# Transposes of queries, keys, attention weights and merged rows by VectorE and DRAM, branch sums kept in PSUM, and a planned SyncE queue

## The chip, the cores and the metric

The kernel runs on one core of one Trainium2 chip. The metric is the device time of one execution in microseconds (us), median of the runs. TensorE (PE in the profile) multiplies matrices into PSUM, ScalarE (ACT) and VectorE (DVE) work on tiles of 128 partitions, GpSimd (POOL) and SyncE (SP) mostly issue transfers (DMA) between DRAM and the on-chip memory (SBUF).

## What is computed

One layer of a gated encoder: 512 tokens of width 2048, float32. All twelve attention heads are of width 128; three branches (A, B, C) have four heads each.

```python
hn = rmsnorm(x, norm_g)
proj = hn @ w_in                 # 2048 x 12292: q, k, v, gate of 12 heads,
                                 # 4 forget logits, 3 x 2048 merge gates
gates = sigmoid(merge columns + b_gate)
ya = softmax(qn kn^T + cumulated log forget, causal) v          # branch A
yb = softmax(qn kn^T + relative bias, 9 chunks of 64) v         # branch B
yc = stick-breaking(q k^T) v                                    # branch C
y  = [ya, yb, yc] * silu(gate)
merged = sum over branches of gates_n * (y_n @ w_up_n)          # 512 x 2048
out = x + merged @ w_out
```

qn and kn are q and k after a root-mean-square norm of each head (A and B only).

## The kernel before

**Products.** Each float32 operand is split into a high part that TensorE's fast format holds exactly and a low remainder (ACT makes the high part, L376, DVE the low, L386). A product is three fast matmuls, high by high, low by high, high by low; every one of them goes through `mm` (L266). A **unit** is the work on one weight tile of 256 rows by 512 columns: 12 matmuls of 128x128 by 128x512. There are 8 raw weight tiles in SBUF (NR), and the splits run LA = 2 units ahead.

**Strassen.** Two groups of 512 columns (one gate group and the q, k, v, gate of one head) are computed together by a seven-product Strassen scheme (class `Strassen`, L596 to L704; each product has 4 units, named by `PLAIN`, in the order 5, 1, 6, 7, 4, 2, 3). The weight sums of products 5 and 7 are made by DMAs that add into the tile (`add_up`, issued by POOL, L282); those of 6 and 3 by DVE (L588). Each product has its own pair of PSUM banks (one for each half of the tokens), of 4 in all (`accs`); four more banks serve attention (`atts`). What comes out is combined by DVE and ACT in SBUF (`after`, L649 to L704).

**Order of the whole.** First two groups (head C0 and gate group 0) are multiplied without Strassen, then 11 Strassen tasks run, one for each further head with a gate group, then the up projection (24 units of 24 matmuls, `up_units`), then the output projection (2 Strassen tasks, `out_task`).

**A head** (class `Head`). Its q, k, v and gate lie token by token and have to be laid out channel by channel: `turned` (L868 to L876) makes 4 TensorE transposes each for K and Q into an `atts` bank, from which ACT and DVE make the split parts (`qk`). The gate of all heads but the last goes another way (`gate`): DVE transposes blocks of 32x32 (L920), SP stores the tile to DRAM (L923), and ACT's queue fetches it back in pieces of 32 floats (L930). The scores (`soft_scores`, `stick_scores`, L261 to L263) are then made; the weights p are transposed on TensorE (`soft_trans`, L1019, 10 blocks a head), split, and multiplied by the values (`av`, L1107 to L1109). For the last head the mask is added by a small matmul (L988) and the steps stand closer together. The finished head is stored (`yd`) and fetched back in the up projection. The merged rows are transposed on TensorE too (`turned_m`, L1357, 4 groups of 16 blocks).

**Forget logits** are made on DVE (`forget_sums`) from x rows and weight rows fetched in 512-column pieces.

**The planner.** `Flow` simulates PE, ACT and DVE while the program is built: each step is a generator that yields events, slots (`t2s`, `atts`, `raws`...) or an engine with a cost; the earliest startable step goes next and steps that could start together go by due time. The three engines carry out their instructions in the order thus written. SP's queue is not planned: `fetch` and `stored` only estimate when a transfer lands (`landing`). `at(u, step)` lets a step begin at unit u; the offsets within a head stand in `OFF`.

Of the kernel before, what the change touches and what calls it, by code (L numbers as in the profile page):

```python
# [36 lines left out]
Q, K, V, G = 0, 1, 2, 3  # L37
PE, ACT, DVE = 0, 1, 2
# [19 lines left out]
class Task:  # L58
    def __init__(self, gen, slack, ready):
        self.gen, self.slack, self.ready = gen, slack, ready  # L60
        self.prev, self.fin = None, 0.0
        self.engine = self.cost = self.due = self.wait = None


class Flow:
# [5 lines left out]
    LATE = (0.3, 0.12, 0.12)  # L71

    def __init__(self):
        self.clock = [0.0] * 3
        self.idle = [0.0] * 3
        self.now = self.fin = 0.0
        self.tasks = []
# [12 lines left out]
    def advance(self, task):  # L90
        while True:
# [16 lines left out]
            elif isinstance(w[0], Slots):  # L108
                slots, n = w
                if len(slots.free) < n + (slots.kept if task.slack > 1 else 0):  # L110
                    return
                slots.free.sort()
                task.ready = max(task.ready, slots.free[n - 1])
# [11 lines left out]
    def run(self):  # L125
        while self.tasks:
            best = None
            for t in list(self.tasks):
                if t.engine is None:
                    self.advance(t)  # L130
            for t in self.tasks:
                if t.engine is not None:
                    key = (max(self.clock[t.engine], t.ready), t.due)
                    if best is None or key < best[0]:
                        best = key, t
# [4 lines left out]
            e = t.engine  # L140
            self.idle[e] += start - self.clock[e]
            self.now = start
# [21 lines left out]
def hybrid_kernel(  # L164
# [22 lines left out]
    pa = ctx.enter_context(tc.tile_pool(name="pa", bufs=4, space=PS))  # L187
    pt = ctx.enter_context(tc.tile_pool(name="pt", bufs=4, space=PS))
# [9 lines left out]
    t2s, atts, raws, xps = Slots(NT, KEPT), Slots(4), Slots(NR), Slots(NX)  # L198
    accs, wls = Slots(4), Slots(LA)
# [69 lines left out]
    line = [0.0, 0.0]  # L269
# [7 lines left out]
    def fetch(to, src, ready, kb):  # L277
        nc.sync.dma_start(to, src)
        return Event(landing(ready, kb))
# [28 lines left out]
    onef, zerof, nu_f = tmpc[:, blk(0)], tmpc[:, blk(1)], tmpc[:, blk(2)]  # L308
# [5 lines left out]
    identb = cp.tile([P, P], BF16, name="identb")  # L314
    nc.vector.tensor_copy(identb, identf)

    mska = cp.tile([P, P], BF16, name="mska")
    nc.gpsimd.affine_select(out=nu_f, in_=zerof, pattern=[[-1, P]], base=0, channel_multiplier=1,
                            compare_op=ALU.is_ge, fill=NEG)
    nc.vector.tensor_copy(mska, nu_f)  # L320

# [6 lines left out]
    for c in (0, 2):  # L328
# [3 lines left out]
    rstd = cp.tile([P, QB], F32, name="rstd")  # L332
    rstd_ev = Event()
# [4 lines left out]
                                                  mybir.EngineType.DVE}))  # L338
# [8 lines left out]
    class Unit:  # L347
# [7 lines left out]
        def load(self):  # L355
            for s in self.srcs:
                yield raws, 1
                self.raw = raw_tile(self.shape)
                self.there.t = fetch(self.raw, s, flow.ready, 256 * self.shape[0]).t
# [30 lines left out]
    def products(u, ps, kts, tbs, block, first=False, last=False, bank=None, done=None, outer=False):  # L390

        for group in [[tb] for tb in tbs] if outer else [tbs]:
            if bank is not None:
                for tb in group:
                    yield bank[0], 1
                    ps[tb] = bank[1]()
            for j, kt in enumerate(kts):
                for tb in group:
# [4 lines left out]
                    mm(ps[tb], h, u.hi[:, j, :], first and j == 0)  # L403
                    mm(ps[tb], lo, u.hi[:, j, :])
            yield u.ready
            for j, kt in enumerate(kts):
                for tb in group:
                    yield PE, mm_us(S)
                    mm(ps[tb], block(kt, tb)[0], u.lo[:, j, :], stop=last and j == len(kts) - 1)
# [75 lines left out]
    def norm_x():  # L485
# [11 lines left out]
        yield from rsqrt(rstd, m, D, tmp, QB)  # L497
        set_(rstd_ev)
# [54 lines left out]
    class Product(Unit):  # L553
# [6 lines left out]
        def load(self):  # L560
# [7 lines left out]
            ev = fetch(self.raw, task.src(*first, c), flow.ready, 512)  # L568
# [23 lines left out]
    PLAIN = [(p, c) for p in (5, 1, 6, 7, 4, 2, 3) for c in range(CH)]  # L592

    class Strassen:
# [9 lines left out]
        def __init__(self, src, ops, done, order=PLAIN, other=(), rest=None):  # L604
            self.src, self.ops, self.done, self.rest = src, ops, done, rest
            self.order, self.other = order, other
            self.ps, self.ev = {}, {}
            self.v, self.u, self.u2, self.u3 = ([None, None] for _ in range(4))
# [8 lines left out]
        def mms_of(self, p, c):  # L617
            own = [x for q, x in self.order if q == p]
            first, last = c == own[0], c == own[-1]
            slots, new = (atts, att) if p in self.other else (accs, acc)  # L620

            def go(u):
                ps = self.ps.setdefault(p, [None, None])
                if first:
                    yield slots, 2
                    ps[:] = new(), new()
                yield from products(u, ps, (2 * c, 2 * c + 1), (0, 1), self.ops[p], first, last,
                                    done=lambda tb: self.after(p, tb, slots), outer=last)
            return go

        def left(self, name, tb, op):
# [6 lines left out]
            yield fetch(r, self.rest(name, tb), flow.now, 256)  # L638
# [5 lines left out]
        def after(self, p, tb, slots):  # L644
            ps = self.ps[p][tb]
            v, u, u2, u3 = self.v, self.u, self.u2, self.u3
# [6 lines left out]
            if p in (1, 5):  # L653
                yield t2s, 1
                c = t2("v" if p == 5 else "u")
                yield ACT, act_us(S)
                nc.scalar.activation(c, ps, AF.Copy)
                (v if p == 5 else u)[tb] = c
                give(slots)
# [914 lines left out]
```

## Time and profile before

| | |
|---|---|
| median of 3 runs | 1300.71 us (1300.23 to 1301.82) |
| the profiled execution's span | 1300.1 us |
| instructions | 17368 |
| granted TensorE clock | 1.000 |
| busy: PE, DVE, ACT, POOL | 1294.1, 1069.5, 748.2, 92.0 us |
| moved by DMA | 284.39 MB |
| matmuls of 512 columns through L266 | 5328 |
| other TensorE instructions | 613 |

Busy time is the union of an engine's instructions. Matmuls are pipelined: one of 512 columns is shown about 390 ns long, but the next starts 227 ns after it. In the chain of what ended last each matmul counts only until the next one starts, so that chain gives the cost of an instruction in the stream. The DMA share is the mean busy share of the core's 16 DMA engines; the queues are q1 (issued by SP), q10 (by ACT) and q0 (by POOL).

### The profile page before, as it was taken

The numbers are of one execution on the slowest core, as the hardware profiler recorded it, in microseconds if no ns is written. First come the engines' busy times: TensorE is split into PE (matmuls) and PEld (weight loads), VectorE is DVE, ScalarE is ACT, GpSimd is POOL, SyncE is SP. The second block draws the span as 40 slices with busy tenths as digits, with TensorE's granted clock in tenths as the row PEclk, the third lists the DMA queues.
The fourth block names the chain that finished last, engine by engine and source line by source line (L and its number), as shares of the span: only waits on it lengthen the run. The fifth ranks groups of instructions, "written<-read, shape, count | busy, mean of one in ns | idle before, by whom it ended". The sixth has DMA issues, their size and how long they took to land.

```text
span 1300.1 us, 17368 instructions
## 1 busy us (share of the span) xinstructions
PE 1294.1 (100%) x5941; PEld 1075.1 (83%) x5941; DVE 1069.5 (82%) x1607; ACT 748.2 (58%) x1259; POOL 92.0 (7%) x116
## 2 busy tenths in 40 slices
PE   9999999999999999999999999999999999999998
PEld 8888888888888888888888888888888888888887
DVE  7966797898989888898886886978879668698767
ACT  7745465565557646576466664666658546463442
POOL 0001000110011001110011000110000000000110
PEclk9999999999999999999999999999999999999999
DMA  9855687896788989888787777877796756738983
GB/s 358 256 147 145 185 230 194 230 239 215 218 238 237 250 236 272 236 240 240 205 249 175 222 213 191 252 162 208 224 282 194 264 194 196 177 93 258 250 245 126
DMA packets 124072, 284.39 MB, mean 219 GB/s; under 512 B 34368, under 2 KB 40144, under 8 KB 123984
## 3 DMA queue, kind: packets, MB, share of 16 engines
q1 hardware_dynamic: 83328, 221.42, 50.7%
q0 software_dynamic: 14976, 54.53, 23.1%
q10 hardware_dynamic: 25680, 7.34, 2.3%
q8 instruction: 46, 0.75, 0.2%
q14 instruction: 42, 0.34, 0.1%
HBM read 260.66 MB, written 22.59 MB: 218 GB/s over the span
## 4 chain that ended last, share of the span: by engine, by line
PE 99%; DMA 1%; DVE 0%; issue 0%; ACT 0%; ACTq 0%
PE acc L266 93%; PE att L1019 1%; PE att L873 1%; DMA gl<-u 1%; PE att L1109 1%; PE att L1108 1%; PE att L261 1%; PE att L262 1%; PE att L263 1%; PE att L1357 1%; PE att L1107 1%; PE att L430 0%; DVE s L702 0%; DVE u L1161 0%; DVE gt L920 0%
## 5 line engine op out<-in xcount | busy, mean ns | idle before, releaser
L376 ACT ACTIVATE wh<-raw 128x1024 fp32r<-128x1024 f32 (+1 forms) x404 | 426.9, 1057 | 412.6 <-PE acc L266 317.6
L386 DVE TENSOR_TENSOR wl<-raw,wh 128x1024 fp32r<-128x1024 f32 (+1 forms) x405 | 492.6, 1218 | 159.1 <-PE acc L266 110.6
L266 PE MATMUL acc<-wh,x 128*128 128x512 f32 x1664 | 428.7, 392 | 0.1
L266 PEld LDWEIGHTS acc<-wh,x 128*128 128x128 f32 x1664 | 310.2, 188 | 62.8 <-issue 0.3
L266 PE MATMUL acc<-wh,t 128*128 128x512 f32 x1056 | 272.4, 391 | 0.0
L266 PE MATMUL acc<-wl,x 128*128 128x512 f32 x832 | 230.7, 391 | 0.0
L266 PEld LDWEIGHTS acc<-wh,t 128*128 128x128 f32 x1056 | 197.1, 188 | 40.3
L266 PEld LDWEIGHTS acc<-wl,x 128*128 128x128 f32 x832 | 155.4, 188 | 32.3 <-DVE wl L386 0.2
L266 PE MATMUL acc<-wl,t 128*128 128x512 f32 x528 | 148.0, 392 | 0.0
L282 POOL DMA_DIRECT2D raw<-in_w_col x88 | 76.1, 865 | 867.6 <-ACT wh L376 209.0
L588 DVE TENSOR_TENSOR raw<-raw,raw 128x1024 f32<-128x1024 f32 x104 | 126.4, 1218 | 0.1
L266 PEld LDWEIGHTS acc<-wl,t 128*128 128x128 f32 x528 | 98.3, 188 | 19.7
L266 PE MATMUL acc<-wh,m 128*128 128x512 f32 x448 | 112.9, 389 | 0.0
L266 PE MATMUL acc<-wh,y 128*128 128x512 f32 x384 | 103.1, 390 | 0.0
L266 PEld LDWEIGHTS acc<-wh,m 128*128 128x128 f32 x448 | 84.1, 188 | 17.4
L266 PEld LDWEIGHTS acc<-wh,y 128*128 128x128 f32 x384 | 72.0, 188 | 15.0
L266 PE MATMUL acc<-wl,m 128*128 128x512 f32 x224 | 62.5, 390 | 0.0
L266 PE MATMUL acc<-wl,y 128*128 128x512 f32 x192 | 59.5, 391 | 0.0
L266 PEld LDWEIGHTS acc<-wl,m 128*128 128x128 f32 x224 | 41.9, 188 | 8.8 <-DVE wl L386 0.2
L266 PEld LDWEIGHTS acc<-wl,y 128*128 128x128 f32 x192 | 35.8, 188 | 7.1
L247 ACT ACTIVATE ah<-att 128x512 fp32r<-128x512 f32 (+3 forms) x48 | 20.9, 436 | 31.7 <-PE att L1019 31.6
L1323 DVE TENSOR_TENSOR sg<-acc,sg 128x512 f32<-128x512 f32 x48 | 32.9, 690 | 5.0 <-PE acc L266 2.6
(182 smaller groups left out, 1119.9 us busy)
## 6 DMA issues: line engine op xcount, KB each, us to landing
raw<-in_w_col SPq DMA_DIRECT2D x235, 512.0 KB, 5.0
raw<-in_w_col POOLq DMA_DIRECT2D x88, 512.0 KB, 8.2
raw<-in_w_out SPq DMA_DIRECT2D x40, 512.0 KB, 4.1
raw<-in_w_up SPq DMA_DIRECT2D x24, 512.0 KB, 3.8
sg<-gl SPq DMA_DIRECT2D x48, 256.0 KB, 4.8
xf<-in_xn SPq DMA_DIRECT2D x32, 256.0 KB, 6.7
raw<-in_w_out POOLq DMA_DIRECT2D x16, 512.0 KB, 6.5
gl<-u SPq DMA_DIRECT2D x22, 256.0 KB, 9.9
```

The costliest lines, as they stand in the source:

```text
L247: nc.scalar.activation(hi, src, AF.Copy)
L261: nc.tensor.matmul(ps, lh, rh, start=start, stop=False, skip_group_check=more)
L262: nc.tensor.matmul(ps, lh, rl, start=False, stop=False, skip_group_check=more)
L263: nc.tensor.matmul(ps, ll, rh, start=False, stop=stop, skip_group_check=more)
L266: nc.tensor.matmul(ps, w, x, start=start, stop=stop, skip_group_check=more)
L282: nc.gpsimd.dma_start(to, src, accum_op=ALU.add)
L376: nc.scalar.activation(u.hi, u.raw, AF.Copy)
L386: nc.vector.tensor_sub(u.lo, u.raw, f(u.hi))
L588: nc.vector.tensor_add(to.raw, to.raw, self.raw)
L873: nc.tensor.transpose(ps[:, blk(tb)], self.c[tb][:, blk(r)], identf)
L1019: nc.tensor.transpose(ps[:, blk(i)], self.p[i][:, blk(j)], identf)
L1323: nc.vector.tensor_mul(t, ps[tb], t)
```

## The change

1. **q, k, gate** of every head go the way the gate went: DVE transposes 32x32 blocks in the 384 columns q, k, gate of each of 4 token tiles (`crossed`), SP stores the four tiles (values with them), and SP fetches K, Q and the gate back, each by four DMAs in pieces of 32 floats (`back`); the values come back by one DMA. `turned` and its TensorE transposes are gone.
2. **Attention weights**: DVE transposes p in place (`sent`), SP stores it, and `soft_in` fetches the four column blocks back by four DMAs each. `soft_trans` is gone.
3. **Merged rows**: groups 0, 2 and 1 of 4 go the same way (`folded`, `turned_m`); the last, 3, stays on TensorE (`spun_m`).
4. **Strassen sums in PSUM**: products 6, 7 and 4 are added by TensorE into the banks that hold product 1, product 3 into those of product 5. ACT copies the bank after 1 and after 6, and the next product on it waits (`gate`) for that copy. Order 5, 1, 6, 7, 2, 3, 4. Banks: 6 `accs`, 2 `atts`.
5. **SP is planned** as a fourth engine: each fetch and store yields SP with a cost, and SP carries out its queue in the planned order. A step takes a slot only when it is free to within 0.5 us.
6. **Order**: heads C0 and C1 come first without Strassen; the last Strassen task holds two gate groups instead of the last head; offsets in a head are longer; the mask matmul is gone. The up projection takes branches A of groups 0 and 2 later.
7. **Forget logits** in 8 pieces of 256 columns, all four heads at once: 32 fetches of 256 KB instead of 48, and 128 DVE sums of 256 columns instead of 64 of 512.

```diff
-    pa = ctx.enter_context(tc.tile_pool(name="pa", bufs=4, space=PS))
-    pt = ctx.enter_context(tc.tile_pool(name="pt", bufs=4, space=PS))
+    pa = ctx.enter_context(tc.tile_pool(name="pa", bufs=6, space=PS))
+    pt = ctx.enter_context(tc.tile_pool(name="pt", bufs=2, space=PS))
...
     def landing(ready, kb):
-        line[0] = max(line[0], ready) + 0.5
-        line[1] = max(line[1], line[0] + 1.0) + kb / 370.0
-        return line[1] + 1.5
+        line[0] = max(line[0], ready + 1.0) + kb / 370.0
+        return line[0] + (LAND if ready > 20.0 else 1.6)
+    def store(to, t, kb, slots=None, n=1):
+        yield SP, 0.37
+        nc.sync.dma_start(to, t)
+        ev = Event(landing(flow.fin, kb))
...
+    def back(to, src):
+        n = src.shape[0] * 4
+        for b in range(4):
+            yield SP, 0.54
+            nc.sync.dma_start(to[32 * b:32 * (b + 1), :].rearrange("p (n c) -> p n c", c=32),
+                              src.rearrange("t (a r) c -> (t a) r c", r=32)[:, :, 32 * b:32 * (b + 1)]
+                              .rearrange("n r c -> r n c"))
+        return Event(landing(flow.fin, n * 32) + PIECES)
     def add_up(to, src, ready, kb):
         nc.gpsimd.dma_start(to, src, accum_op=ALU.add)
-        line[1] += kb / 250.0
-        return Event(max(line[1], ready) + 6.5)
+        line[0] += kb / 250.0
+        return Event(max(line[0], ready) + 6.5)
...
+            opens = p in (5, 1, 2)
+            key = {3: 5, 6: 1, 7: 1, 4: 1}.get(p, p)
+            after = {6: 1, 7: 6, 3: 5, 4: 7}.get(p)
             def go(u):
+                ps = self.banks.setdefault(key, [None, None])
+                gate = (lambda tb: self.event(after, tb)) if first and not opens else None
...
+            if p in (1, 6):
                 yield t2s, 1
+                t = (u if p == 1 else u2)[tb] = t2("u")
                 yield ACT, act_us(S)
+                nc.scalar.activation(t, w, AF.Copy)
                 set_(self.event(p, tb))
...
+        def crossed(self):
...
+            for tb in range(QB):
+                yield DVE, dve_us(3 * P) + 0.07
+                c = self.c[tb]
+                nc.vector.transpose(c[:, :3 * P], c[:, :3 * P])
+                ev = yield from store(d[tb], c, 256, t2s)
+            self.event("x").t = ev.t + LATER
+        def qk_in(self, r):
+            yield self.event("x")
...
+            yield (yield from back(t, self.d[:, :, blk(r)]))
+            if self.n == C:
+                yield from split(h, lo, t, S)
...
+        def sent(self, i):
+            yield self.event("s", i)
...
+            nc.vector.transpose(p, p)
+            self.gone[i] = (yield from store(self.pd[i, :, :m], p, m / 2)).t
+        def soft_in(self, j):
+            for i in range(j, QB):
+                yield self.event("d", i)
+            yield Event(max(self.gone) + LATER)
...
+            yield (yield from back(f(lo), self.pd[j:, :, blk(j)]))
+            yield from split(h, lo, f(lo), n, self.event("a", j))
...
-OFF = dict(cs=4, ct=12, co=14, s=8, t=14, o=16, s1=3, t1=4, o1=5)
-FAT, FGAP, FLATE = 44, 15, 3.5
+UPS = [(0, 0), (0, 1), (2, 0), (2, 1), (0, 2), (2, 2)] + [(g, b) for g in (1, 3) for b in range(3)]
+DRAMS = (0, 2, 1)
+EARLY = 0.5
+LAND, PIECES = 2.5, 1.5
+OFF = dict(sc=12, tc=20, oc=22, s=12, t=20, o=22)
+LATER = 2.5
+FAT, FGAP, FLATE, FSLACK = 24, 20, 3.5, 4.0
```

More of the change, by code (lines that the diff above doesn't have):

```diff
@@ L36 @@
 A, B, C = 0, 1, 2
-Q, K, V, G = 0, 1, 2, 3
-PE, ACT, DVE = 0, 1, 2
+Q, K, G, V = 0, 1, 2, 3
+PE, ACT, DVE, SP = 0, 1, 2, 3
 MARGIN = 0.25
@@ L61, in __init__ @@
         self.prev, self.fin = None, 0.0
-        self.engine = self.cost = self.due = self.wait = None
+        self.engine = self.cost = self.due = self.wait = self.until = None
 class Flow:
-    LATE = (0.3, 0.12, 0.12)
+    LATE = (0.3, 0.12, 0.12, 0.0)
     def __init__(self):
-        self.clock = [0.0] * 3
-        self.idle = [0.0] * 3
+        self.clock = [0.0] * 4
+        self.idle = [0.0] * 4
         self.now = self.fin = 0.0
@@ L396, in products @@
                     ps[tb] = bank[1]()
+            if gate is not None:
+                for tb in group:
+                    yield gate(tb)
             for j, kt in enumerate(kts):
@@ L619, in mms_of @@
             first, last = c == own[0], c == own[-1]
-            slots, new = (atts, att) if p in self.other else (accs, acc)
+            opens = p in (5, 1, 2)
+            key = {3: 5, 6: 1, 7: 1, 4: 1}.get(p, p)
+            after = {6: 1, 7: 6, 3: 5, 4: 7}.get(p)
             def go(u):
[L623 to L628, printed above, removed]
+                ps = self.banks.setdefault(key, [None, None])
+                gate = (lambda tb: self.event(after, tb)) if first and not opens else None
+                if first and opens:
+                    yield accs, 2
+                    ps[:] = acc(), acc()
+                yield from products(u, ps, (2 * c, 2 * c + 1), (0, 1), self.ops[p], first and opens, last,
+                                    done=lambda tb: self.after(p, tb), outer=last or gate is not None, gate=gate,
+                                    more=True)
             return go
@@ L1348, in hybrid_kernel, with folded, arrived, spun_m @@
     kept_m, m1_ev, mus = {}, [Event() for _ in range(UK)], {}
-    def turned_m(g, i):
+    md = {}
+    def folded(g, tb):
+        yield merged_ev[NB - 1, g, tb]
+        m = merged[g, tb]
+        yield DVE, dve_us(S) + 0.07
+        nc.vector.transpose(m, m)
+        if g not in md:
+            md[g] = dp.tile([QB, P, S], F32, name=nm("md"))
+        md_ev[g, tb].t = (yield from store(md[g][tb], m, 256, t2s)).t + LATER
+    md_ev = {(g, tb): Event() for g in range(NQ) for tb in range(QB)}
+    def turned_m(g, i):
+        for tb in range(QB):
+            yield md_ev[g, tb]
+        yield t2s, 1
+        m = t2("m")
+        yield (yield from back(m, md[g][:, :, blk(i)]))
+        arrived(g, i, m)
+    def arrived(g, i, m):
+        k = 4 * g + i
+        if k < UK:
+            kept_m[k] = m
+            spawn(merged_a(k, m), 4.0, flow.fin)
+        else:
+            spawn(merged_b(k - UK, m), 3.0, flow.fin)
+    def spun_m(g, i):
         for tb in range(QB):
@@ L1454, in out_task @@
             order += PLAIN[2 * CH:]
-        return Strassen(src, mops, done, order, other, rest).units
+        return Strassen(src, mops, done, order, rest).units
     for i in range(2):
```

524 lines of the change are left out of this document (244 added, 280 removed).

## The prediction, on record before the changed kernel ran

> **What bounds the kernel now.** First the page: the engines' totals, the 40 slices, and the chain of work that ended last.
>
> ```profile
> span 1300.1 us, 17368 instructions
> PE 1294.1 (100%) x5941; PEld 1075.1 (83%) x5941; DVE 1069.5 (82%) x1607; ACT 748.2 (58%) x1259; POOL 92.0 (7%) x116
> PEclk9999999999999999999999999999999999999999
> DMA  9855687896788989888787777877796756738983
> PE 99%; DMA 1%; DVE 0%; issue 0%; ACT 0%; ACTq 0%
> ```
>
> TensorE is busy from end to end at full clock, and the chain lies on it for 99%. A microsecond of its work taken out is a microsecond won, unless TensorE then waits for something. DMA, at 0.7 to 0.9 in most slices, stands nearest to being the next bound. The chain in order of time, with its shares by line, gives the price of each kind of instruction in the stream:
>
> ```profile
> by line: PE acc L266 92.5%; PE att L1019 1.0%; PE att L873 0.8%; DMA gl<-u 0.8%; PE att L1109 0.6%; PE att L1108 0.6%; PE att L261 0.6%; PE att L262 0.6%; PE att L263 0.6%; PE att L1357 0.5%; PE att L1107 0.5%; PE att L430 0.3%; issue 0.1%;
> ...
> 5.25 50.91 PE acc L266 x220
> ...
> 747.42 0.44 PE att L873 x4
> ...
> 829.70 0.44 PE att L873 x4
> ...
> 999.12 0.07 PE att L988
> ...
> 1144.18 1.75 PE att L1357 x16
> 1145.93 150.40 PE acc L266 x663
> 1296.33 0.02 issue
> ```
>
> A 512-column matmul costs 150.40/663 = 0.2269 us, a transpose 1.75/16 = 0.109, a mask matmul 0.07. The stream runs from 5.25 to 1296.33, 1291.1 us. The 5328 big matmuls take 1208.7, 285 transposes 31.1, and scores and value products (L261 to L263, L1107 to L1109, together 3.5% of the span) 45. Some 6 us are left over: true waits. A task with its head lasts 829.70 - 747.42 = 82.3 us; without its 18 transposes, 80.3.
>
> **TensorE's part of the sum.** The groups by line give the counts.
>
> ```profile
> L1019 PE MATMUL att<-identf,p 128*128 128x128 f32 x120 | 20.9, 272 | 0.0
> L873 PE MATMUL att<-identf,v 128*128 128x128 f32 x46 | 8.8, 273 | 0.0
> L873 PE MATMUL att<-identf,w 128*128 128x128 f32 x46 | 8.8, 272 | 0.0
> L1357 PE MATMUL att<-identf,sg 128*128 128x128 f32 x64 | 7.6, 273 | 0.0
> L873 PE MATMUL att<-identf,c 128*128 128x128 f32 x8 | 1.2, 272 | 0.0
> L988 PE MATMUL att<-mska,identb 128*128 128x128 bf16 x4 | 0.9, 230 | 0.0
> ```
>
> Removed: 120 for attention weights, 100 for q, k and the last gate, 48 of 64 for merged rows (three groups of four), 4 masks: 268 x 0.109 + 4 x 0.07 = **29.5 us**. Nothing is added: the two plain groups, the 11 + 2 Strassen tasks and the up units keep all 5328 matmuls, in another order and other banks. With the old 6 us of waits the span would be 1270.6, and since the median stands 0.6 above the profiled execution, the time **1271.2 us**; with no wait at all, 1265.
>
> **DVE and ACT.** Strassen's `after` loses L666, L675, L679 and, in the 11 paired tasks, the subtraction of product 4.
>
> ```profile
> L679 DVE TENSOR_TENSOR s<-s,v 128x512 f32<-128x512 f32 x26 | 18.0, 692 | 0.9
> L666 DVE TENSOR_TENSOR s<-u,acc 128x512 f32<-128x512 f32 x26 | 17.8, 686 | 6.3 <-PE acc L266 5.8
> L675 DVE TENSOR_TENSOR w<-s,acc 128x512 f32<-128x512 f32 x26 | 17.8, 684 | 1.1 <-PE acc L266 0.2
> L257 DVE SCALAR_TENSOR_TENSOR w<-w,acc 128x512 f32<-128x512 f32 x22 | 14.1, 681 | 0.0
> L920 DVE STREAM_TRANSPOSE gt<-w 128x128 f32<-128x128 f32 x20 | 6.1, 304 | 0.0
> L657 ACT ACTIVATE u<-acc 128x512 f32<-128x512 f32 x26 | 15.5, 595 | 9.9 <-PE acc L266 9.9
> ```
>
> That is -67.7, and with the gate's 44 transposes of 0.304, -81. New are 48 transposes 384 wide, 12 each of 128, 256, 384 and 512 for the weights, and 12 of 512 for merged rows. The trace has none so wide; the bounds are a sum of the same width (0.69 at 512) and as many times 0.304 as there are blocks. I take the lower, nearer to the rows because the cost of starting an instruction is paid once: +60 (upper end +95). The forget sums, twice as many at half the width, add some 17, the values' split saves 5. In all -9 (to +26) on 1069: DVE's 18% of idle time covers it, cost nothing. ACT gets 26 more bank copies of 0.595 (+15) and loses merged copies and small value splits (-14): nothing.
>
> **Banks.** Products 6 and 7 wait for ACT's copy of the bank to which they add: 13 tasks x 2 boundaries x 2 halves = 52 waits on TensorE, each with the whole stream queued behind it. The timeline's end and the list of waits price one.
>
> ```profile
> 1294.80 1.07 PE L266 MATMUL acc<-wh,m 128*128 128x512 f32 x4
> 1295.00 0.69 DVE L702 TENSOR_TENSOR s<-s,acc 128x512 f32<-128x512 f32 x1 [2.80 <-PE acc L266]
> ...
> ACT wh L376 <- PE acc L266: 317.6, 203, 5.7
> ...
> ACT wh L376 <- DMA raw<-in_w_col: 41.0, 22, 3.7
> ```
>
> A reader of a bank starts 0.20 after the next matmul; the copy takes 0.595. Meanwhile TensorE has the other half's 6 matmuls, 1.36 us, so each wait has 0.5 us to spare. A weight split on ACT (1.06 us, L376) started just before takes that and up to 0.5 more: bounds 0 and 52 x 0.5 = 26 us. I take 1, nearer to nothing, since ACT spends 317.6 us waiting for TensorE before just those splits. The Trainium skill, "Perfetto Trace Analysis", Optimizing Tensor Performance, Matmuls, speaks against this part: independent groups should rotate through banks so that the eviction of one lies beside the next. By it the whole 0.8 us would be exposed; no run so far shows such a wait.
>
> **Transfers.** Each head now makes two round trips through DRAM ahead of TensorE: products, norm, DVE transpose, store, `back`, split, **scores**; then softmax, transpose, store, `back`, split, **value products**. 24 junctions at which TensorE, in order, stands still if a transfer lands later than the planner assumed. The cover is the offsets in the diff: K and Q are asked for 4 and 3 units (2.7 us each) before the scores, the weights 2 units before the values. On SP a store waits for DVE, and a `back` for its store; queued behind are weight loads, for which ACT's splits wait. The views, in this order: the queues over one task (700 to 782 us), over 62 to 64 us, the packets at the start (20 to 40 us), two windows (next to last number: DMA share), the issues with their time to landing.
>
> ```profile
> q1 hardware_dynamic: 4407, 12.58, 47.2%
> q0 software_dynamic: 1070, 3.89, 26.0%
> q10 hardware_dynamic: 2112, 0.26, 2.0%
> ...
> q0 software_dynamic: 113, 0.40, 114.2%
> ...
> DMA packets 3260, 7.83 MB, mean 392 GB/s; under 512 B 363, under 2 KB 363, under 8 KB 3258
> ...
> 500.00:600.00 100.00, 100.00 (x466) 83.28 (x464) 86.45 (x154) 58.04 (x106) 7.76 (x9) 1.00 0.89 254
> 700.00:800.00 100.00, 100.00 (x461) 83.19 (x460) 75.44 (x106) 56.24 (x98) 7.44 (x9) 1.00 0.75 200
> ...
> gd<-gt SPq DMA_DIRECT2D x11, 256.0 KB, 11.6
> g<-gd ACTq DMA_DIRECT2D x44, 64.0 KB, 2.9
> tb<-in_rel SPq DMA_DIRECT2D x4, 256.0 KB, 10.5
> ```
>
> A small piece (q10) takes 2.0% of 82 x 16 engine-us over 2112 packets, 12.4 ns; large packets go at 12.58 MB in 47.2%, 20.3 B/ns an engine. A head gains 11264 - 2048 = 9216 pieces (114 engine-us) and 1.7 MB of stores and value fetches (84): 198/16 = 12.4 us. One task now uses 75.4% of 82 = 61.8, so 74.2 of the 80.3 us that a task would last: 92%. Beside the forget logits (0.89 in their window) it is 73.0 + 12.4, less 4.6 (the forget part fetches 1.05 MB every 20 units, not 1.57 every 15): 80.8, just full. At the start's rate (392 GB/s, 24.5 B/ns) the large packets shrink by a sixth, so it still fits. Landing times are the risk: with q0 alone on the engines (an adding DMA, over 100% of 62 to 64) a transfer behind it waits, and plain fetches took 10.5 us to land where the planner reckons some 4. Bounds for a junction: 0 and 5 us; I take 0.2 on average, near nothing, since the values' fetches fall on units 20 to 23 with no adding DMA due, and the diff's constants allow 6.7 us for a store and 6.4 for a `back`, against 2.9 for a quarter of one: 24 x 0.2 = 4.8, call it 4.
>
> SP's own issues (28 of about 0.5 us and 11 of 0.33 a head, 18 of 80 us) fit. Two `atts` instead of four only let scores, values and forget sums begin later in the plan, which fills TensorE with big matmuls meanwhile: nothing, or another part of the junctions' bounds if a bank is held longer than planned. The last head now lies under a whole task of two gate groups (some 76 us) before the up projection needs it, where its steps stood close together: nothing, and the cover is three times a head's length from scores to values (10 units, 27 us). The end is as before: one subtraction and a store behind the last product. Sum: 1271.2 + 1 + 4 = **1276 us**.
>
> **Rivals.**
>
> *Late transfers eat much of it* (1281 to 1298). Landings late by 0.4 to 1.1 us at each of 24 junctions give +10 to +27. For: 10.5 us landings, full DMA beside the forget logits. Against: the loads are spread, and TensorE waited only 6 us in all so far.
>
> *Banks* (1281 to 1297): a weight split is usually ahead of the copy, 52 x 0.2 to 0.5. Against: ACT is mostly idle there. With all 0.8 exposed, 42 us, it would be 1313.
>
> *DMA becomes the bound, slower.* In the six heads beside the forget logits demand is already 80.8 for 80.3. If pieces on SP's queue cost X instead of 12.4 ns, a task's transfers take 72.1 + 0.704 X there (11264/16 pieces), 65.5 + 0.704 X elsewhere. The other 24.7 us of gain are gone when six tasks last 4.1 us longer than 80.3, from X = 17 ns on (28 at the start's rate). At 20 ns they last 5.9 longer, 35 in all: about 1311. For: mixed traffic. Against: 12.4 measured amid weight loads.
>
> The Trainium skill, "VectorE: DVE Perf Modes", The three transpose paths, calls a plain DMA copy with strides for a transpose 19 times slower than the crossbar's. If that held for these pieces (19 x 6.3 ns = 120, an estimate from that page, with the large-packet rate in the crossbar's place) every task's transfers would last 150 us or more, the kernel over 2000; the trace's 12.4 disagrees, because DVE has turned the 32x32 blocks and 128 bytes lie together.
>
> *It does not do what it says*: something else already paces TensorE, so that removed transposes reappear as waits: 1298 to 1303. Against: 6 us of waits, clock at full.
>
> **Chances.** Forecast, 1266 to 1281: 0.55. Late transfers 0.20, banks 0.05 (both 1281 to 1298). No change 0.05. DMA bound 0.15 (0.01 of it by the 19-fold rule). Range 1266 to 1298, 0.80; its low end is TensorE without waits, its high end takes in both middle rivals. Within 0.2% (2.6 us) is what a measurement of this kernel can't tell from no change: faster 0.80, same 0.05, slower 0.15.
>
> **What would show it.** TensorE instructions 5941 - 272 = 5669; transposes 17 (16 merged, 1 forget). The chain still 98% or more on TensorE, big matmuls at 0.227. Bank waits: idle before L266 released by ACT's bank copy, under 3 us in all. Late transfers: idle before L261 or L1107 released by ACT or DVE, and before these by DMA. DMA bound: the share near 1.0 over stretches of 100 us and ACT's L376 waiting for raw far over its present 41 us. The forecast is wrong if junction waits pass 10 us, if loads starve the splits, or if pieces cost over 17 ns.

## The result and the profile after

The changed kernel takes 1352.1 us (median of 4 runs, 1345.4 to 1354.8) where the one before takes 1301.3 (4 runs): a ratio of 1.038, interval 1.036 to 1.041. It is slower by 51 us. The forecast was 1276 us, the range 1266 to 1298, so both the size and the sign were wrong.

The page of the changed kernel: totals, granted clock and DMA share in 40 slices, packets, the two large queues, and the weight loads (number, KB, median us from issue to landing); the last line is the weight loads of the kernel before. PEld is TensorE's loading of the operand that stays in it during a matmul.

```profile
span 1349.0 us, 17631 instructions
PE 1293.2 (96%) x5669; PEld 1055.1 (78%) x5669; DVE 1047.2 (78%) x1662; ACT 751.7 (56%) x1236; POOL 91.5 (7%) x115
PEclk9999999999999999999999999999999999989999
DMA  9848989979879999997898989999898878947983
DMA packets 284893, 322.20 MB, mean 239 GB/s; under 512 B 178544, under 2 KB 197632, under 8 KB 284800
q1 hardware_dynamic: 267376, 262.08, 63.7%
q0 software_dynamic: 14976, 54.53, 21.7%
raw<-in_w_col SPq DMA_DIRECT2D x235, 512.0 KB, 6.5
...
raw<-in_w_col SPq DMA_DIRECT2D x235, 512.0 KB, 5.0
```

TensorE has the 5669 instructions that were forecast, 272 fewer than before, but it is busy for 96% of the span instead of 100%, and its mean granted clock is 0.988. The chain of what ended last no longer helps (its shares add up to 23% of the span), so the list of waits is the view to read: who waited for whom, us in total, times, longest. In it raw is a weight tile as loaded, wh and wl are its two split parts, u is a bank copy and sg a merge gate. The stores in DRAM are qd (queries, keys, gate, values), pd (attention weights) and md (merged rows). The last two lines are all that TensorE waited for in the kernel before.

```profile
ACT wh L402 <- DMA raw<-in_w_col: 61.6, 32, 8.6
...
PEld acc L278 <- DVE wl L412: 32.2, 27, 4.3
...
ACT vh L259 <- DMA vl<-qd: 24.2, 8, 9.1
...
PE acc L278 <- DVE wl L412: 20.7, 17, 3.9
...
DVE m L1405 <- DMA m<-md: 17.1, 5, 5.3
PEld acc L278 <- ACT wh L402: 15.8, 12, 3.6
...
PE acc L278 <- ACT wh L402: 10.9, 8, 3.1
...
PE acc L278 <- ACT u L699: 4.8, 3, 2.4
...
PE att L1114 <- ACT ah L259: 4.5, 4, 1.7
...
PE acc L278 <- DVE sg L1326: 4.2, 1, 4.2
...
PE att L430 <- DVE mskf L302: 1.1, 1, 1.1
PE att L261 <- ACT p L1049: 0.9, 1, 0.9
```

TensorE's own waits add up to 51 us (2.0 before). Most are not at scores (L273 to L275) or value products (L1114 to L1116), where the forecast looked: those are 9.4 us. They are at the big matmuls (L278), which wait for the two halves of a split weight tile (wh, wl). The engines that make these halves had waited for transfers: ACT for weight loads and values, DVE for merged rows. Both work strictly in their written order, so a late transfer holds every split written behind it. One place, in the timelines of ACT and TensorE (start, length, instruction, idle before and what ended it):

```profile
366.85 0.63 ACT L259 ACTIVATE vh<-vl 128x512 fp32r<-128x512 f32 x1 [3.75 <-DMA vl<-qd]
367.38 1.06 ACT L699 ACTIVATE u<-acc 128x512 f32<-128x512 f32 x2
368.34 1.06 ACT L402 ACTIVATE wh<-raw 128x1024 fp32r<-128x1024 f32 x1
...
368.02 2.07 PE L278 MATMUL acc<-wh,t 128*128 128x512 f32 x4 [2.42 <-ACT u L699]
```

A head's values land 3.75 us late. ACT stands before their split; written behind it are two bank copies (u) and a weight split. TensorE has run out of what does not need those banks and stands for 2.42 us. The values themselves are not what TensorE wanted.

All of TensorE's waits can be followed back in these timelines: from a wait to the engine that ended it, on that engine to its last idle time, and so on to what ended that. Of the 51 us, 45 end so at a transfer: 27 at rows that come back from DRAM (queries, keys, values and gate 10.9, merged rows 10.4, attention weights 4.5, finished heads 1.6), 9 at weight loads, 8 at merge gates, forget pieces and other rows. This reads the order of events alone and leaves slack in between out of account, but by it the round trips, more than the weight loads, stand at the start of the waits.

What follows the wait above is in windows of the same trace (PE, PEld, DVE, ACT, POOL busy with counts, granted clock, DMA share, GB/s). The share adds up the times of packets, so it passes 1 where packets overlap on an engine.

```profile
365.60:368.00 2.40, 0.00 (x0) 0.00 (x0) 0.49 (x1) 1.15 (x3) 0.00 (x0) 0.95 1.10 310
368.00:370.00 2.00, 1.98 (x5) 1.60 (x6) 2.00 (x5) 1.83 (x4) 0.00 (x0) 0.50 1.03 276
370.00:372.00 2.00, 2.00 (x9) 1.67 (x8) 0.86 (x3) 0.00 (x0) 0.86 (x1) 0.70 1.04 404
372.00:374.00 2.00, 2.00 (x10) 1.62 (x9) 1.27 (x5) 1.84 (x5) 0.00 (x0) 1.00 1.03 385
...
298.91:307.48 8.57, 6.53 (x29) 5.07 (x27) 3.56 (x4) 0.00 (x1) 0.00 (x0) 1.00 0.62 240
420.92:424.58 3.66, 3.66 (x18) 3.04 (x17) 2.52 (x4) 0.16 (x1) 0.87 (x1) 1.00 1.07 247
483.28:488.54 5.26, 5.26 (x25) 4.18 (x23) 2.96 (x3) 0.00 (x0) 0.00 (x0) 1.00 1.07 234
771.39:780.50 9.11, 7.96 (x36) 6.25 (x34) 2.35 (x2) 0.01 (x1) 0.00 (x0) 1.00 1.04 225
...
100.00:960.00 860.00, 826.05 (x3614) 671.30 (x3613) 693.58 (x1156) 505.82 (x866) 69.02 (x80) 0.99 0.91 243
```

The first four rows: after the wait TensorE runs at half clock for more than 2 us. Over the span the clock costs (1 - 0.988) x 1349 = 16 us, nearly all of it in nine stretches at half clock of 3.4 us each. The next four are long waits of ACT for transfers: in three the DMA engines are busy throughout (share 1.04 to 1.07). In the longest wait for a weight tile (8.57 us) they are not (0.62): two broadcasts of forget weights (fb) had been issued just ahead, and loads were late although engines had room. The last row covers the heads; the same stretch before, in the same view:

```profile
100.00:960.00 860.00, 859.05 (x3950) 714.02 (x3949) 724.92 (x1097) 506.80 (x857) 72.48 (x84) 1.00 0.80 221
```

The DMA share rose from 0.80 to 0.91, and TensorE was busy 33 us less in it.

Of the 87 us between the 1265 us of a TensorE without any wait and the measured time, the listed waits (51) and the clock (16) name 67. The other 20 no row names, but the start times of the matmuls in the trace place them. Some 7 belong to the same waits: a matmul is shown 0.39 us long and the next could start after 0.227, so the beginning of a wait is hidden. Some 9 are delays of mostly under 0.2 us between big matmuls; the kernel before has as many (8.9), and the 6 us of waits that the prediction found in it are mostly these. The rest lies at the small matmuls.

### The profile page after: what moved, and what is told of

The parts are those of the page before. It is cut to its first block, busy times and chain, and to the rows that moved or that the text cites. A ratio compares the mean times of both kernels' runs of the same rounds, so it can differ in the third digit from the quotient of the medians.

```text
span 1349.0 us, 17631 instructions
## 1 busy us (share of the span) xinstructions
PE 1293.2 (96%) x5669; PEld 1055.1 (78%) x5669; DVE 1047.2 (78%) x1662; ACT 751.7 (56%) x1236; POOL 91.5 (7%) x115
## 3 DMA queue, kind: packets, MB, share of 16 engines
q1 hardware_dynamic: 267376, 262.08, 63.7%
## 5 line engine op out<-in xcount | busy, mean ns | idle before, releaser
L278 PE MATMUL acc<-wh,x 128*128 128x512 f32 x1664 | 427.4, 392 | 8.7 <-ACT wh L402 8.6
L278 PEld LDWEIGHTS acc<-wh,x 128*128 128x128 f32 x1664 | 312.3, 189 | 76.4 <-ACT wh L402 12.4
L278 PE MATMUL acc<-wh,t 128*128 128x512 f32 x1056 | 279.0, 394 | 7.1 <-ACT u L699 4.8
L278 PE MATMUL acc<-wl,x 128*128 128x512 f32 x832 | 235.3, 394 | 7.7 <-DVE wl L412 7.4
L278 PEld LDWEIGHTS acc<-wh,t 128*128 128x128 f32 x1056 | 199.8, 190 | 50.7 <-ACT u L699 6.3
L278 PEld LDWEIGHTS acc<-wl,x 128*128 128x128 f32 x832 | 155.6, 189 | 46.1 <-DVE wl L412 14.8
L278 PE MATMUL acc<-wl,t 128*128 128x512 f32 x528 | 156.1, 394 | 3.1 <-DVE wl L412 2.9
L278 PEld LDWEIGHTS acc<-wl,t 128*128 128x128 f32 x528 | 99.2, 189 | 25.4 <-DVE wl L412 5.2
L278 PE MATMUL acc<-wh,m 128*128 128x512 f32 x448 | 116.4, 394 | 0.0
L278 PE MATMUL acc<-wh,y 128*128 128x512 f32 x384 | 105.2, 396 | 4.2 <-DVE sg L1326 4.2
L278 PEld LDWEIGHTS acc<-wh,m 128*128 128x128 f32 x448 | 85.5, 191 | 18.1
L278 PEld LDWEIGHTS acc<-wh,y 128*128 128x128 f32 x384 | 73.5, 192 | 20.2 <-DVE sg L1326 4.6
L278 PE MATMUL acc<-wl,m 128*128 128x512 f32 x224 | 65.3, 397 | 4.8 <-DVE wl L412 4.8
L278 PE MATMUL acc<-wl,y 128*128 128x512 f32 x192 | 60.8, 398 | 5.6 <-DVE wl L412 5.6
L278 PEld LDWEIGHTS acc<-wl,m 128*128 128x128 f32 x224 | 42.4, 190 | 14.3 <-DVE wl L412 5.7
L699 ACT ACTIVATE u<-acc 128x512 f32<-128x512 f32 x52 | 30.9, 597 | 39.3 <-PE acc L278 39.0
L780 DVE CUSTOM_DVE_ANT_0 att<-xf,fb 128x256 f32<-128x256 f32 x96 | 41.0, 428 | 12.6 <-DMA xf<-in_xn 9.8
L278 PEld LDWEIGHTS acc<-wl,y 128*128 128x128 f32 x192 | 36.6, 192 | 13.9 <-DVE wl L412 6.5
```

What stands on the lines that cost most here:

```text
L278: nc.tensor.matmul(ps, w, x, start=start, stop=stop, skip_group_check=more)
L699: nc.scalar.activation(t, w, AF.Copy)
L780: nc.vector.tensor_tensor_reduce(out=xi if h == NH - 1 else o[:, :HS], in0=xi, in1=two(ws[h // 2])[:, h % 2, :], scale=1.0, scalar=0.0, op ...
```

## The experiments

Three theories. **T1**: the transfer engines are close to full, transfers land late, ACT and DVE stand before them in order, weight splits come late and TensorE starves. **T2**: SP, now in planned order, stands before a store or a fetch, and weight loads behind it are issued late. **T3**: the sums in PSUM, with their order and their two attention banks, cost time by themselves. All times are medians beside runs of the kernel before on the same chip; brackets give the ratio to it with its interval.

**No adding DMAs** (products 5 and 7 use weights that are not summed).

```diff
-        nc.gpsimd.dma_start(to, src, accum_op=ALU.add)
```

> The changed kernel without its 104 adding DMAs (products 5 and 7 use unsummed weights); the plan, every queue's order and all else stay. Theory T1 (the transfer engines are nearly full, transfers land later than planned, ACT and DVE wait for them in order, the weight splits behind them come late and TensorE starves): the engines lose the 21.7% of their time that queue q0 takes, the waits of ACT for raw tiles and fetched-back rows mostly go, 1270 to 1290 us. Rival T2 (SyncE's planned queue is blocked by stores and fetches-back that wait, and so weight loads are issued late): the queue's order is unchanged, so over 1330 us. Rival T3 (sums in PSUM, and the order 5 1 6 7 2 3 4): bank waits are unchanged, but the loads of 5 and 7 get shorter; 1300 to 1340.

Measured 1294.2 us [0.994, 0.992 to 0.995]: 58 less than the changed kernel. Its largest row of TensorE's waits, and the heads in its windows:

```profile
PE acc L278 <- DVE wl L411: 9.0, 7, 3.6
```

```profile
100.00:960.00 860.00, 855.15 (x3823) 705.93 (x3822) 731.79 (x1197) 533.59 (x903) 0.00 (x0) 1.00 0.73 206
```

This is 4 us above the range of T1 and outside those of the rivals. With the share at 0.73, TensorE's wait for DVE is 9.0 us instead of 20.7, and ACT's for weight loads falls from 61.6 to 23.9. This is T1's direction, but not a clean proof: a summed tile is also ready earlier when it need not be added to. The adding DMAs are in both kernels; the 38 MB that the change adds came on top of them.

**Long runs**: rows come back in pieces of 128 floats instead of 32, so the data stands in another layout, with as many DMAs and as many bytes.

```diff
-            nc.sync.dma_start(to[32 * b:32 * (b + 1), :].rearrange("p (n c) -> p n c", c=32),
-                              src.rearrange("t (a r) c -> (t a) r c", r=32)...
+            nc.sync.dma_start(to[32 * b:32 * (b + 1), :].rearrange("p (t c) -> p t c", c=P),
+                              src[:, 32 * b:32 * (b + 1), :].rearrange("t r c -> r t c"))
```

> The changed kernel with each fetch-back cut into runs of 128 floats instead of 32 (same bytes and number of DMAs; the rows come back in the wrong layout). T1: three quarters of some 144 thousand pieces go; at about 14.6 ns each for the small and 28 for the larger ones that frees some 68 us of each transfer engine, and the time falls by 10 to 30 us, to 1320 to 1342. T2 and T3: within 5 us of 1350.

Measured 1329.6 [1.022, 1.018 to 1.025], 22.5 less. From the page:

```profile
DMA packets 165085, 322.20 MB, mean 243 GB/s; under 512 B 18800, under 2 KB 77824, under 8 KB 164992
...
q1 hardware_dynamic: 147568, 262.08, 61.3%
```

q1's time on an engine fell from 63.7% of 1349.0 (859 us) to 61.3% of 1326.2 (813): 46 us of some 1170 that an engine works for all queues, where 68 had been expected. The order, the bytes and the number of DMAs are the same, so this is the clean test that the transfers' own time costs TensorE time: 4% less work for the transfer engines is worth 22 us. Whether fuller engines or longer single trips are to blame it does not separate, because the trips became shorter too (median landing of a quarter of K or Q 4.4 us instead of 5.1; of a weight load 6.2 instead of 6.5). Followed back as above, the waits that begin at returning rows fall from 27 to 14 us, and those that begin at weight loads do not fall (9, then 14).

**SP not planned.**

```diff
-                                                  mybir.EngineType.DVE, mybir.EngineType.SP}))
+                                                  mybir.EngineType.DVE}))
```

> The changed kernel with SyncE left out of the engines whose order is written by hand, as before the change; the plan of the other three is the same. T2: the time falls below 1325. T1: the same bytes in the same stretches, 1340 to 1365. T3: as T1.

Measured 1348.4 [1.036, 1.028 to 1.044]: as the changed kernel. ACT's waits for weight loads more than doubled (132.8 us), yet TensorE's list stays at 49. The planned order of SP is not the cause, so T2 as stated falls; and ACT's waits are no measure of the loss by themselves.

**Parts taken back.** In each, TensorE transposes that operand again (`nc.tensor.transpose` into an att bank) and the rest stays. `all_pe` takes back weights, q, k and merged rows, with the old offsets in a head; gate and values still go through DRAM, and sums, order, banks and planned SP are the new ones.

```diff
-DRAMS = (0, 2, 1)
+DRAMS = ()                      # merged rows
...
+            for tb in range(QB):    # q, k
+                nc.tensor.transpose(ps[:, blk(tb)], self.c[tb][:, blk(r)], identf)
...
+            for i in range(j, QB):  # attention weights
+                nc.tensor.transpose(ps[:, blk(i)], self.p[i][:, blk(j)], identf)
```

All three:

> The changed kernel with queries, keys, attention weights and all merged rows transposed on TensorE again, at the offsets within a head of the kernel before; the gate and the values still travel through DRAM; sums in PSUM, planned SyncE, order of the whole and forget pieces stay as changed. T1: transfer share back to about 0.75, TensorE has its 29 us of transposes again and hardly waits: 1295 to 1308. T2: SyncE's queue has fewer blocking entries, 1300 to 1320. T3: all bank waits and the new order stay, over 1320.

Attention weights only:

> The changed kernel with the attention weights alone transposed on TensorE again (120 transposes, 13.1 us of stream more; 61 thousand pieces and 15.7 MB fewer). T1: 1310 to 1335, with the transfer share down by some 0.05 and fewer half-clock stretches. Other theories: 1350 plus 13, about 1360.

Merged rows only:

> The changed kernel with all merged rows transposed on TensorE (48 transposes, 5.2 us of stream more). T1: the waits of DVE for fetched merged rows, and TensorE's four waits between 1135 and 1195 us (10.4 us, and two or three stretches at half clock) go: 1337 to 1346. Others: 1352 to 1358.

q and k only:

> The changed kernel with queries and keys alone transposed on TensorE again (96 transposes, 10.5 us of stream more; 49 thousand pieces and 12.6 MB of fetches and 12.6 MB of stores fewer). T1 (full transfer engines, late transfers): 1310 to 1335, as for the attention weights. If only the attention weights' trips hurt: 1350 to 1362.

Weights and merged rows:

> The changed kernel with attention weights and all merged rows on TensorE; queries and keys still go through DRAM. T1: the two gains add up (30 and 10 us below the changed kernel): 1308 to 1316. If they share one cause that either removal cures: about 1320.

Measured, with the sum of TensorE's listed waits, ACT's wait for weight loads, and the DMA share from 100 to 960 us:

| kernel | us | ratio | TensorE waits | ACT for loads | DMA share |
|---|---|---|---|---|---|
| before | 1301.3 | 1 | 2.0 | 41.0 | 0.80 |
| changed | 1352.1 | 1.038 (1.036 to 1.041) | 51 | 61.6 | 0.91 |
| merged rows back | 1341.6 | 1.031 (1.027 to 1.035) | 43 | 60.7 | 0.93 |
| q, k back | 1321.1 | 1.015 (1.013 to 1.017) | 29 | 52.5 | 0.89 |
| weights back | 1321.1 | 1.015 (1.012 to 1.018) | 26 | 55.0 | 0.86 |
| weights, merged back | 1317.6 | 1.013 (1.011 to 1.015) | 18 | 57.9 | 0.86 |
| all back | 1318.4 | 1.013 (1.008 to 1.018) | 14 | 30.5 | 0.80 |

Putting 120 transposes of weights back adds 13.1 us of work to TensorE, and the time still falls by 31; q and k add 96 x 0.109 = 10.5, and it falls by 31 as well (they are 6.3 MB of stores and 6.3 of fetches, half of what the forecast of that run says). They do not add up: with all three back it falls by 34. Counted with the work that TensorE takes back (13.1, 10.5 and 5.2 us), the reliefs are 44, 42 and 16, and 63 for all three, so part of the cause is shared. A price that rises steeply near full use would do that, but it is not shown: the kernel with all three back also has the old offsets in a head, and the cost of part 4 may be a floor under all of them.

With everything back 17 us remain, more than T1 allowed (1295 to 1308): the rest of the change costs time too. Only the range of T2 holds this time, and T2 has fallen. For weights and merged rows together the sum of the two gains (1308 to 1316) was missed and the forecast of a shared cause, about 1320, came nearer.

**Sums in PSUM alone**: the kernel before with the new `Strassen` and `products`, order 5, 1, 6, 7, 2, 3, 4, banks 6 and 2; then the same in the old order.

```diff
-    pa = ctx.enter_context(tc.tile_pool(name="pa", bufs=4, space=PS))
-    pt = ctx.enter_context(tc.tile_pool(name="pt", bufs=4, space=PS))
+    pa = ctx.enter_context(tc.tile_pool(name="pa", bufs=6, space=PS))
+    pt = ctx.enter_context(tc.tile_pool(name="pt", bufs=2, space=PS))
...
-for p in (5, 1, 6, 7, 4, 2, 3) for c in range(CH)
+for p in (5, 1, 6, 7, 2, 3, 4) for c in range(CH)
```

> The kernel before with nothing of the change but the Strassen sums in PSUM (with the order 5 1 6 7 2 3 4 and the banks 6 and 2). T1 (late transfers): TensorE does the same work and DVE has less, 1298 to 1303. T3 (waits for the bank copies and the new order cost): 1305 to 1325, with waits of L266 for ACT's bank copies.

> The kernel before with the Strassen sums in PSUM, but the old order 5 1 6 7 4 2 3. If e5's loss comes from the order (product 4, and with it the last quarter of the head, ends at the task's last unit, so that norms and transposes of q and k are late): 1299 to 1306. If it comes from the sums in PSUM as such (bank copies, fewer banks for attention): 1312 to 1325.

Measured 1319.0 (only two runs, 1315.2 and 1322.9) [1.014, 1.007 to 1.021] in the new order, 1308.7 [1.006, 1.004 to 1.008] in the old. Waits of the first, then of the second:

```profile
PEld att L886 <- ACT v L878: 7.4, 15, 1.3
...
PE att L886 <- ACT v L878: 4.3, 8, 1.1
...
PE acc L266 <- DVE sg L1336: 2.0, 1, 2.0
```

```profile
PE att L261 <- DVE mx L1008: 2.5, 3, 0.9
PE att L261 <- DVE fl L760: 1.6, 1, 1.6
```

T3 holds in part, and not where the forecast had looked: no row of either list has TensorE waiting for a bank copy (u). With product 4 last, the transposes of q and k (L886) wait for ACT's norm, which now comes at the very end of a task. In the old order that is gone, and what is left are scores (L261) that are released by the reader of an attention bank: there are two banks where there were four. The second time lies between its two ranges, so both reasons have a share. In the kernel before, then, part 4 costs some 18 us by itself (9 to 27 by the interval), some 10 of it by the order; that the two banks are the other 7 is read from the releasers (4.1 us in the two rows shown), not tried. How much of the 18 is left in the changed kernel, with its longer offsets, is not shown.

**Planning for later landings.** If transfers are only later than the plan says, telling it so should help; if room is short, it can't. `late_plan` tells it of all transfers, `late_back` only of the fetches back and the values.

```diff
-LAND, PIECES = 2.5, 1.5
+LAND, PIECES = 5.0, 3.0
...
-        line[0] += kb / 250.0
-        return Event(max(line[0], ready) + 6.5)
+        line[0] += kb / 150.0
+        return Event(max(line[0], ready) + 8.0)
```

```diff
-        return Event(landing(flow.fin, n * 32) + PIECES)
+        return Event(landing(flow.fin, n * 32) + PIECES + 4.0)
```

> The changed kernel with a planner that is told of later landings: fetches and stores land 2.5 us later than it reckons now, fetches-back another 1.5, an adding DMA takes 512/150 us of the line instead of 512/250 and lands 1.5 later. Same work, same bytes. If lateness against the plan is the cause (T1a), ACT and DVE wait less with split work behind them: 1295 to 1335. If the transfer engines' capacity is (T1b), nothing is to be had by order: 1340 to 1360.

> The changed kernel with only the fetches-back and the values' fetch planned to land 4 us later; weight loads, stores and adding DMAs stay as reckoned. If the fault is ACT and DVE standing in order before rows that have not come back, with weight splits queued behind (T1c), they stand less: 1320 to 1340. If it is the weight loads themselves, slow to land in nearly full engines and limited by eight raw tiles (T1d): 1345 to 1360, with ACT's waits for raw tiles as before.

Measured 1368.1 [1.051, 1.048 to 1.054] and 1362.1 [1.047, 1.043 to 1.051]: both slower than the changed kernel, and outside every range (the second by 2 us from that of T1d). Waits of the first:

```profile
PE acc L278 <- DVE sg L1326: 15.5, 3, 7.9
...
PE acc L278 <- ACT u L699: 10.2, 3, 6.2
```

ACT's wait for weight loads fell (45.1), but TensorE's list rose to 61: bank copies and gates came late instead. In the second, ACT's wait for weight loads rose (71.6), and so did TensorE's list (59). Here a later plan moves the waits; it does not make room. That it holds tiles longer and so delays what follows is argued, not shown. Which transfers carry most of the loss, the rows that come back or the weight loads behind them, these two runs did not tell; the waits followed back in the changed kernel's trace point to the rows.

**The kernel before with merged rows of two groups through DRAM**, three ways: all 16 fetches at once; one unit apart and told to land 8 us later; and the fetch written as an own step of ACT's plan, so that it stands behind its stores.

```diff
+DRAMS = (0, 2)
...
+    def folded(g, tb):
...
+        nc.vector.transpose(m, m)
...
+        nc.sync.dma_start(md[g][tb], m)
...
+    def fetched_m(g, i):
...
+        yield t2s, 1
+        yield ACT, 0.05                                # third only
...
+        ev = Event(landing(flow.now, 512) + 8.0)       # second: + 16.0; third: flow.fin + 14.0
...
+                at(len(units), lambda g=g, i=i: fetched_m(g, i))    # second, third: len(units) + 1 + i
```

> The kernel before with nothing but merged groups 0 and 2 of four going through DRAM (32 transposes off TensorE, 3.5 us of stream), where the transfer share is 0.55 to 0.7 and fetches have 30 us and more to land. T1: with room on the transfer engines the gain stays: 1296.5 to 1299, a ratio of 0.9965 to 0.999. If trips through DRAM cost TensorE time wherever they are: 1302 or more.

> As e11 (the kernel before, merged groups 0 and 2 through DRAM), but the four fetches of a group are begun one unit apart instead of all at once, and each is planned to land 8 us later still. If e11 lost because 16 fetches in a row on SyncE's queue held up the gates' and weights' loads behind them (SPq 1047 to 1057 us) and DVE stood before rows not yet there: 1297 to 1300, the 3.5 us of transposes less. If any such trip costs: over 1305.

> As e14, but a fetch of merged rows is first planned as a short step of its own after the stores, and the rows are reckoned to land 14 us after that step; e14's plan counted from the time at which the step was begun and let DVE stand 7 us before them (trace at 1045 to 1052 us). If waiting in order for rows planned too early was all of e14's loss: 1296.5 to 1299.5, the 3.5 us of transposes less. If a trip through DRAM costs TensorE time even with room on the engines and a late plan: over 1302.

Measured 1316.6 [1.012, 1.010 to 1.013], 1310.4 [1.007, 1.005 to 1.008] and 1297.4 [0.997, 0.996 to 0.998]. SP's timeline of the first, then its waits:

```profile
1047.07 9.66 SPq L1370 DMA_DIRECT2D m<-md  x16
1056.78 0.96 SPq L278 DMA_DIRECT2D sg<-gl  x2
```

```profile
PE acc L266 <- DVE sg L1323: 8.7, 2, 5.6
PE acc L266 <- ACT m L247: 5.5, 1, 5.5
```

The 32 transposes (3.5 us) went as they should, and the detour cost 19: 9.66 us of issues stood ahead of the gates that the up projection needed, and DVE stood 22 us before the fetched rows; which of the two cost more is not separated. Spread out, it still lost 9 us. The third won 3.4 of the 3.5. DVE shows why, here in the second:

```profile
1052.03 0.42 DVE L1408 TENSOR_TENSOR m<-m 128x256 f32<-128x256 f32 x1 [7.06 <-DMA m<-md]
```

In the third the first rows are used no earlier, at 1052.15, but DVE had stood only 1.17 us before them and had carried out four gate products in the meantime. SP issues the fetches of both at about the same times (from 1047.63 and 1047.68). So what cost time in the second was not the trip here, but DVE standing before it with other work behind. The page of the third:

```profile
PE 1290.4 (100%) x5909; PEld 1070.4 (83%) x5909; DVE 1072.4 (83%) x1615; ACT 744.1 (57%) x1251; POOL 91.8 (7%) x116
PEclk9999999999999999999999999999999999999999
```

This version beats both kernels, by 0.28% over the one before.

## Why the prediction was wrong, point by point

**TensorE's part of the sum: as forecast.** The instructions are the 5669 forecast, and the price of 0.109 held where it was tried alone: in the kernel before, 32 transposes less gave 3.4 us of 3.5.

**DVE and ACT: right.** DVE's busy time fell by 22.3 us (1069.5 to 1047.2), more than the forecast 9, and ACT's rose by 3.5. The wide transposes cost what the lower bound said, in the groups by shape:

```profile
L1015 DVE STREAM_TRANSPOSE p<-p 128x512 f32<-128x512 f32 x12 | 8.4, 703 | 2.7 <-ACT p L1077 2.6
L905 DVE STREAM_TRANSPOSE v<-v 128x384 f32<-128x384 f32 x20 | 11.2, 563 | 0.0
```

"Cost nothing" for these engines' busy time was right, but said nothing of when they are held.

**Banks: right on the copy, wrong on the part.** Where the sums were tried alone no bank copy held TensorE. The Trainium skill, "Perfetto Trace Analysis", Optimizing Tensor Performance, Matmuls, advises that independent groups rotate through banks. The prediction worked out that by this 0.8 us would be exposed at each of 52 boundaries; the two traces with the sums alone show no such wait. In the changed kernel three waits for bank copies (4.8 us) come up, over the 3 us that the prediction allowed as a sign, the one shown behind a late transfer. Missed was the rest of part 4: the order and the two attention banks, costed at "nothing, or another part of the junctions' bounds", took about 18 us by themselves in the kernel before.

**Transfers: the demand was right, its price was the step that failed.** The forecast was 92% of a task for the DMA engines, and just full beside the forget logits. The share over the heads, 0.91, is no direct test of that, because TensorE's waits made the heads longer; the total work of the engines is. The queues of the kernel before, from its page (packets, MB, share of 16 engines):

```profile
q1 hardware_dynamic: 83328, 221.42, 50.7%
q0 software_dynamic: 14976, 54.53, 23.1%
q10 hardware_dynamic: 25680, 7.34, 2.3%
```

With the small queues these are 76.4% of 1300.1, 993 us for an engine; after it is 86.6% of 1349.0, 1168, so 175 more. Twelve heads at the forecast's 12.4 are 149, and by the same prices the merged rows add 29 and the forget part takes away some 13: 165. The term that failed is "I take 0.2 on average, near nothing" for each of 24 junctions (4.8 us, which the sum has as 4), with the reasoning that a demand below the task's length fits; beside the forget logits even its own demand was 80.8 us for 80.3. In place of these 4 us the trace has 51 us of waits and 16 of clock. The term was mis-sized and misplaced. Misplaced: junction waits are 9.4 us, below the 10 set as a limit, but every late transfer also holds ACT or DVE in front of weight splits, and there TensorE lost the most; "if loads starve the splits" was in the list of what would prove it wrong, without a price. Mis-sized: lateness is not bounded by one landing of 5 us at 24 places. It acts on the weight loads too (median landing 6.5 instead of 5.0 us), and nine waits of 1.7 to 4.2 us each brought a stretch at half clock besides, 16 us in all.

Nor does lateness need full engines. From 1060 to 1210 us, in the up projection, the share was only 0.78, and TensorE stood 10.4 us there behind merged rows; with merged rows back on TensorE it had no wait in that stretch.

**Rivals.** "Late transfers eat much of it" had the cause, but looked for it at the junctions and priced it at 27 us at most; with the clock, late transfers ate all of the gain and more (what part 4 adds to that is open). "DMA becomes the bound, slower" needed 17 ns a piece and a share near 1.0 over 100 us. Neither came (13.9 ns on average for the 128-byte packets of q1, and at most 0.95 over 100 us), and yet the kernel is slower: transfers do not need to be the bound to cost time. This rival was the only way to a slower kernel that the prediction saw (0.15). By the same 13.9 ns the rival of 19 times the price played no part.

## What to carry to other kernels

Price a transfer by who stands in order behind the engine that waits for it, not by whether the DMA engines can carry it: here, at a DMA share of 0.91 over the heads, loads landed late, and an engine that was free on average was held just when TensorE needed its next operand. Moving work from TensorE to DRAM round trips paid here in one place, where the rows were used late enough behind their fetch: two groups of merged rows in the kernel before (3.4 us won from 32 transposes, share 0.73 from 1040 to 1180 us). Three groups in the changed kernel cost 10.5, in the same part of the work at a share of 0.78. A change that alters the order of products should be costed for what waits on the last of them, too.

## What the runs showed of the hardware

A wait on TensorE can cost more than its length. After 2.42 us of idle time (the first windows rows above) the granted clock was 0.50 for 2 us and 0.70 for the next 2. The Trainium skill, "TensorE: Matmul & The Clock Gate", Part 1: The HAM clock gate, describes a free-running window of about 3.4 us and a halved clock after an idle one; its table of rules under Why this matters for your kernels asks for no idle gaps over some 3 us. The halving agrees; here a shorter gap was enough. The window agrees as well: in the changed kernel's trace each of the nine stretches at half clock lasts 3.41 us, and they begin whole multiples of 3.413 us apart. The waits before them were 1.7 to 4.2 us long, while one of 2.77 us, which ended at 782 us, brought none, so the length of a wait alone did not decide it.

The second: transfers can be late while the engines are not full. In the wait of 8.57 us the share was 0.62, and two broadcasts in pieces of 1 KB lay ahead. That these keep only some of the 16 engines busy, behind which every load waits, is argued from that share and not tried.
